# A two-block transformer on one core: tiles moved to multiples of 512 bytes in a partition

## The chip, the core and the metric

The kernel runs on one core of one Trainium2 chip. The metric is the device time of one execution in microseconds (us). The kernel before was timed three times: 1878.39 us median, 1877.34 to 1884.4 us.

Five engines are spoken of: PE (TensorE, matrix products), DVE (VectorE), ACT (ScalarE), POOL (GpSimd) and SP (SyncE, which here only issues loads). A tile in SBUF has 128 partitions; its address in this text is the byte at which it begins within a partition, and its *residue* is that address modulo 512.

## What is computed

256 tokens of 1024 channels pass through two blocks of two layers each, all in float32. Cut to what matters:

```
# first block: h = rms_norm(x) * (1 + scale(c)) + shift(c);  x = x + gate(c) * layer(h)
#   layer 0  retention:   q, k, v, g = split(h @ ret_w_in);  ... @ ret_w_out
#   layer 1  forgetting attention, 16 heads:  split(h @ fox_w_in);  ... @ fox_w_out
# second block: x = layer_norm(alpha * x + layer(x)) * g + b
#   conformer conv:  a, gate = split(x @ w_in);  u = a * sigmoid(gate)
#                    silu(layer_norm(depthwise_conv(u, 31 taps) + b)) @ w_out
#   dense ffn:       (silu(x @ w_gate) * (x @ w_up)) @ w_down               # 1024 -> 2816 -> 1024
#   short conv:      b, c, h = split(x @ w_in);  (b * depthwise_conv(c * h, 3 taps)) @ w_out
#   experts:         gates = softmax over the 2 chosen of 8 experts
#     for e in range(8):
#         h = silu(x @ w_gate[e]) * (x @ w_up[e])                           # 1024 -> 3584
#         out = out + gates[..., e:e+1] * (h @ w_down[e])                   # 3584 -> 1024
```

Of some 500 MB that are read, 352 MB are the weights of the eight experts (8 x 3 x 1024 x 3584 x 4 bytes).

## The kernel before

**Streamed weights.** The class `Stream` loads the weights in the order of their use, in units of 1 MB (a raw tile of 128 x 2048 float32), into rings of buffers. Each unit is split into two tiles of type fp32r, whose sum is the float32 value: ACT copies raw to `wH` with rounding (L122), DVE subtracts, `wL = raw - wH` (L123). There are three buffers of each. In the experts ten raw buffers run ahead: three in each of the pools "w", "w2" and "moe0" and one more.

**Three passes for a product.** `mm3` (L231 to L233) issues three matmuls for every product of 128 x 128 by 128 x N: high by high, low by high, high by low. A matmul has a *stationary* operand of 128 columns (512 bytes in each partition), which PE loads with LDWEIGHTS, and a *moving* operand of N columns that streams past it. In the profile's rows `mm<-wH,xg` the moving operand stands first, the stationary second. Each matmul of `mm3` loads its own stationary operand.

**Which operand is stationary** is decided by the stage. In `proj_wst` the weights are (`mm<-hH,wH`, N = 256). In the others the activations are, and the weights move with N = 512: `hH`, `hL` (first projections), `roH`, `foH` (outputs of the first block), `cR` (output of the conformer), `gH`, `gL` (dense down-projection), `soH`, `soL` (output of the short conv), and in the experts `xg`, `hT` or `hH` for gate and up, and `mhH`, `mhL` for down. The tokens of expert e lie in the tile `("xg", "hT", "hH")[e % 3]` (L1329): `xg` in the pool "moe" for experts 0, 3 and 6, the long-lived tiles `hT` and `hH` for the other five.

**One step of the experts** is 512 of the 3584 inner columns: 24 matmuls for the gate, 24 for up, 24 for down (of the columns before) and 4 transposes; there are 7 steps in each of 8 experts, and a step takes in six units. Between two experts `slots_back` carries rows back to their tokens. A second pass over the experts, under a condition, isn't run with these inputs.

**Where tiles lie.** Nothing in the kernel says an address. Pools lie behind each other in the order in which they are opened, and tiles within a pool in the order in which they are first asked for, each size rounded up to 32 bytes. So the sizes of the small tiles of the pool `cp` (`cv` L433, `cst` L436, `v` L475) set where every later pool begins, and small tiles at the start of "conf" (`cst`, L1099) and "moe0" (`rl`, `rmask`, `rpos` in `router_tiles`) set where the tiles behind them begin. Addresses of the built program, with the residue in brackets:

```
tile                                    address (residue)
cst (constants; identity at its start)  17824 (416)
x                                       23680 (128)
raw in "w", "w2", "tmp"                 40064 (128) and on, all 128
wH, wL                                  64640 (128) and on, all 128
hT, hH, hL, xn                          113792 (128) and on, all 128
roH, roL, foH, foL                      189056 (128), 167040 (128) and on, all 128
gH, gL                                  183424 (128) and on, all 128
cR (three buffers)                      183616 (320), 192832 (320), 202048 (320)
cW (three buffers)                      211264 (320), 215360 (320), 219456 (320)
oh, identR, raw in "moe0"               179552 (352), 181600 (352), 183136 (352) and on
soH, soL                                207712 (352), 215904 (352)
xg, ohT, mhH, mhL                       209760 (352), 217952 (352), 221024 (352), 225120 (352)
fxT, fv, fp, fpT (attention)            192, 64, 192 and 320 modulo 512
```

**What sets the order.** A scheduler orders the instructions of each engine by dependence and by the order of the code; loads keep the order of their units on SP's queue, and a load is issued once its raw buffer is free.

Of the kernel before, what the change touches and what calls it, by code (L numbers as in the profile page):

```python
# [6 lines left out]
F32 = mybir.dt.float32  # L7
# [7 lines left out]
P = 128  # L15
# [50 lines left out]
class Stream:  # L66
    """Weights in the order of their use: 1 MB loads run ahead as far as the rings of raw tiles
    allow, then each is split exactly into two parts that fp32r passes carry."""

    def __init__(self, K, split_bufs, pieces=2):  # L70
        self.K, self.SB, self.pieces = K, split_bufs, pieces
        self.units, self.raws, self.parts = [], {}, {}
        self.rings = []
        self.i = self.nl = self.ns = 0
        self.native = None
        self.side = {}
        self.after = 0      # units whose split stays behind what has been traced so far

    def beside(self, fn):
        """fn issues loads of its own in front of the next unit's."""  # L80
        self.side.setdefault(len(self.units), []).append(fn)

    def ring(self, pool, tag, bufs, upto=1 << 30):
        """Buffers for the raw units before unit upto."""
        self.rings.insert(0, [pool, tag, bufs, 0, upto])
# [50 lines left out]
    def ahead(self, n, behind=True):  # L136
        """Splits the next n units, behind what has been traced so far."""
        self.after = max(0, self.i + n - self.ns) if behind else 0
        self._split(self.i + n)

    def get(self, key, hold=0):
        """The next unit; hold: units got before that are still to be used."""
        k, _, split = self.units[self.i]
        assert k == key, (k, key)
        if self.native is not None:
            self.native[3] -= 1
            self.native = None
        self._split(self.i + 1)
        ahead = 0
        j = self.i + 1  # L150
        while j < len(self.units) and ahead < self.SB - 1 - hold:
            ahead += self.units[j][2]
            j += 1
        self._split(j)
        self._load()
        r = self.parts.pop(self.i)
        self.i += 1
        if not split:
            self.native = r[1]
            return r[0]  # L160
        return r
# [31 lines left out]
class Kern:  # L193
# [9 lines left out]
    def table(self, func, after):  # L203
        """Has ACT load func's table off the critical path, once `after` is there."""
        self.nc.scalar.activation(self.t(self.sp, [P, 1], "tab", bufs=2), after, func)

    def ld(self, dst, src):
        """A load that keeps its place among those of the weights."""
        self.tc.keep_in_program_order(self.nc.sync.dma_start(out=dst, in_=src))

    def soon(self, n=400):
        """What is traced inside goes ahead of work traced up to n instructions before."""
        return self.tc.high_priority(n)
# [21 lines left out]
    def behind(self, ins, prev):  # L235
        """ins goes after prev on their engine."""
        self.tc.add_manual_dep(ins.ins, prev.ins.name,
                               mybir.DependencyInfo(mybir.DependencyClass.NoSync, mybir.DependencyReason.DATA),
                               reason="order")

# [1 line left out]
    def proj_tok(self, key, after=None, begun=False):  # L242
        """[t, 512] per token tile, from two units of four k blocks; begun: by first_tok."""
# [11 lines left out]
    def first_tok(self, key):  # L255
        """The first token tile's part of the first unit of a phase."""
# [4 lines left out]
    def proj_wst(self, key, hH, hL):  # L261
        """[n, t] for two blocks of 128 n, from one unit of eight k blocks."""
# [9 lines left out]
    def first_half(self, key):  # L272
        """The first token tile's part of a phase's first product, which needs nothing of the second tile."""
        self.fps = self.mm()
        self.fw = self.st.get(key, 2)
        self.first_tile(0)
# [11 lines left out]
    def proj_two(self, key, key2, begun, between):  # L288
        """Two products as of proj_wst; between takes the first, returns the second. begun: by first_half."""
# [20 lines left out]
    def out_k2(self, key, acc, oH, oL, ks, first, last):  # L310
        """acc[tt][nh] += o[k block].T @ w rows, one unit of two k blocks; oH(k, tt) an AP."""
# [8 lines left out]
    def out_k4(self, key, acc, oH, oL, ks, nh, first, last):  # L320
        """The same for one half of n, one unit of four k blocks."""
# [7 lines left out]
    def out_last(self, key, acc, oH, oL, parts):  # L329
        """The last two units of a product, a token tile at a time; parts: (k blocks, nh, first, last) of each."""  # L330
# [32 lines left out]
    def rpow(self, src, n, eps, scale=1.0, tag="rstd"):  # L363
        """(src * scale + eps) ** -0.5 for a [128, n] AP."""
# [7 lines left out]
    def ln_stats(self, parts, eps):  # L372
        """mean and rstd ([128, 1] each) over the free axis of a list of [128, 512] APs."""
# [11 lines left out]
    def new_h(self, f=True, parts=True):  # L385
        """Channels by tokens, [128, 8, 256]: f32 and the two parts of it."""
# [4 lines left out]
    def turned(self, x, tt, nh):  # L391
        """x.T of one token tile and half of the channels: [128, 4, 128] in a bank."""
# [8 lines left out]
    def plain(self, x, tt):  # L401
        """Token tile tt of x into hT or hH and hL."""
# [9 lines left out]
    def affine(self, x, tt, A, B, f, H, L, func=AF.Identity):  # L412
        """func(A*x.T + B) of token tile tt, and its parts; A, B: [128, 8]."""
# [16 lines left out]
    def setup(self, tmp):  # L430
        nc, a = self.nc, self.a
        cp = self.cp
        cv = cp.tile([P, 8], F32, name="cv")  # L433
        nc.scalar.dma_start(out=cv, in_=a["c"].rearrange("o (p k) -> p (o k)", k=8))
        self.x = self.t(self.xp, [P, 2, DM], "x", bufs=2)
        self.c = c = cp.tile([P, C_MAIN], F32, name="cst")  # L436
# [33 lines left out]
    def vectors(self):  # L470
        """The vectors along partitions."""
# [3 lines left out]
        self.v = self.cp.tile([P, 2 * P], F32, name="v")  # L475
        self.nc.vector.tensor_copy(self.v, ps[:, 0:2 * P])
# [9 lines left out]
    def mod_start(self, parts):  # L486
        """Bias of four chunks of 512 columns, one per 32 partitions, and the sums' bank."""
# [20 lines left out]
    def shift_scale(self, m, i):  # L508
        """m: chunks shift lo, shift hi, scale lo, scale hi -> A = g*(1+scale), B = shift, [128, 8]."""
# [13 lines left out]
    def gate_row(self, m, i):  # L523
        """m: chunks gate0 lo, hi, gate1 lo, hi -> row i spread over the partitions, [128, 1024]."""
# [9 lines left out]
    def residual(self, acc, gate, tt):  # L534
        """x + gate * acc of token tile tt, and rsqrt of its mean square."""
# [216 lines left out]
    def fox(self):  # L752
# [3 lines left out]
        with self.tc.tile_pool(name="fox", bufs=1) as fp:  # L756
# [11 lines left out]
            def decay(ps):  # L768
                """log forget gates, [t, 16] per token tile."""
# [24 lines left out]
            def running(lf):  # L794
                """Their running sums."""
# [14 lines left out]
            def qk(key, g, is_q, begun=False):  # L810
                """Normed heads with the decay's columns: [t, head, 64 | 2] per token tile."""
# [30 lines left out]
            gq, gk = self.v[0:66, P + 24:P + 25], self.v[0:66, P + 25:P + 26]  # L842

            def stage_t(d):
                """Transposed q and k of one head, with the gains."""
# [35 lines left out]
            def stage_v(d0, d1):  # L881
                """o.T of two heads into oT[:, pair, :]."""
# [87 lines left out]
    def rows(self, g, b):  # L970
        """Vectors along the free axis, spread over the partitions."""
# [5 lines left out]
    def deepnorm(self, acc, gb, first, f=False, parts=True):  # L977
        """x = LN(alpha*x + acc)*g + b and its transposed parts; first() follows those of the first token tile."""
# [26 lines left out]
    def conv_rows(self):  # L1005
        """Tap rows by tap mod 4, the upper half of the channels 32 partitions further on, and the
        first 256 channels' as they are from partition 64 on."""
# [11 lines left out]
    def conv_weights(self):  # L1019
        """Taps as [tap mod 4 and channel, group of 32 channels, tap block], and by channel, [128, 2, 31]."""  # L1020
# [14 lines left out]
    def conformer(self):  # L1035
        nc = self.nc
        hH, hL = self.hH, self.hL
        with self.tc.tile_pool(name="conf", bufs=1) as cp:
# [60 lines left out]
            st = self.t(cp, [P, 2, 4, 6], "cst", bufs=1)  # L1099
# [10 lines left out]
            def taps_apart(k, js):  # L1110
                """A block of channels, tap by tap."""
# [76 lines left out]
    def short_conv(self):  # L1188
        nc = self.nc
        hH, hL = self.hH, self.hL  # L1190
        with self.tc.tile_pool(name="sc", bufs=1) as sp:
            oH = sp.tile([P, 8, T], F32R, name="soH")
            oL = sp.tile([P, 8, T], F32R, name="soL")
            wv = self.v[:, P:P + 24].rearrange("p (j k) -> p j k", j=3)
# [29 lines left out]
    def router_tiles(self, pool):  # L1224
        t = lambda n, *sh: pool.tile([P, *sh], F32, name=n)
        self.rl = t("rl", 2, 8)
        self.rt = t("rmask", 2, 8), t("rpos", 3, 8)
        self.oh = self.t(pool, [P, 2, 2, P], "oh", F32R, bufs=1)

    def route(self, tt):  # L1230
        """Router of one token tile: which two experts."""
# [27 lines left out]
    def slots(self, tt):  # L1259
        """The slots of one token tile in the first two experts."""  # L1260
# [15 lines left out]
    def counts(self):  # L1276
        """Tokens of each expert."""
# [15 lines left out]
    def route_weights(self, pool):  # L1293
        """Softmax over the two chosen logits, zero elsewhere; the largest count as an integer."""
# [23 lines left out]
    def gather_steps(self, es, base, oh=None, bank=None):  # L1318
        """Slots base..base+127 of the tokens of two experts: transposed parts per expert, and
        the one-hot rows that carry slots back to tokens; five steps, the last yields them."""  # L1320
# [34 lines left out]
    def experts(self, st, base):  # L1355
        """All experts over their slots base..base+127; adds their gated rows to self.o."""
# [46 lines left out]
        def down_last(e, HL):  # L1403
            """The last rows of the last expert, half of the columns at a time."""
# [25 lines left out]
        def slots_back(e, nh, yHL):  # L1430
            """The slots' rows at their tokens, of half of the columns."""
# [18 lines left out]
        def dense_gates():  # L1450
            """The first gates of the first expert, for all tokens: needs no routing."""
# [12 lines left out]
        def dense_gather(h, HLs):  # L1464
            """The rows of the first expert's slots."""
# [55 lines left out]
    def rest(self):  # L1521
        """Gates, alpha * x and the largest count."""
# [117 lines left out]
    def startup(self):  # L1640
        """The first block's input, half of the channels at a time, and with each half the products that it allows."""
# [143 lines left out]
```

## Time and profile before

| | |
|---|---|
| median of three runs | 1878.39 us (1877.34 to 1884.4) |
| the profiled execution, first to last instruction | 1873.6 us |
| PE busy | 1809.3 us (97%) |
| DVE busy | 1415.0 us (76%) |
| ACT busy | 1064.7 us (57%) |
| mean granted clock of TensorE | 0.986 |
| HBM read | 504.28 MB, 270 GB/s over the span |
| the experts, from their first product to the last | 824 to 1859 us |

The profiled execution is 4.8 us shorter than the median; what lies before the first and behind the last instruction is in the median and not in the span.

How to read it: busy time of PE is made of ends that are modelled, so a matmul's own duration tells little of how fast matmuls follow each other. That is read from their starts in the timeline: the start of the last of a run of matmuls, less the start of the first, by the number of gaps between them. In the timeline a column is the start, the next the modelled duration.

### The profile page before, as it was taken

Reading aid. Unit: us, or ns where it says so; the run is one execution under the profiler, and the core shown is the slowest. Engines: PE = TensorE matmul, PEld = TensorE weight load, DVE = VectorE, ACT = ScalarE, POOL = GpSimd, SP = SyncE. Lnnn points to the kernel's source line nnn. Section 1 sums busy time; section 2 is a strip of 40 time slices with the busy share of each in tenths; the row PEclk is TensorE's granted clock in tenths of the full one; section 3 lists DMA queues with packets and bytes.
Section 4 is the critical chain, followed back from the end, with each engine's and each line's share of the span. In section 5 each row is a group of like instructions: output and inputs, shape, how many; then the busy total and the mean of one; then the engine's idle time right before and its main releaser. Section 6 shows DMA issues by size and latency. Waiting matters only on the chain. (4 is left out here: it accounts for less than half of the span.)

```text
span 1873.6 us, 24361 instructions
## 1 busy us (share of the span) xinstructions
PE 1809.3 (97%) x9741; PEld 1486.5 (79%) x9741; DVE 1415.0 (76%) x1469; ACT 1064.7 (57%) x1036; POOL 65.7 (4%) x112
## 2 busy tenths in 40 slices
PE   6999999999999999999999999999999999999996
PEld 3867778789689998987878878878778788788785
DVE  3656666667775557679888888888888888888887
ACT  3333445654443433347767767767767677677673
POOL 1000003001100001000000000000000000000000
PEclk9999999999999999999999999999999999999998
DMA  9677646237356557548999989999999999999991
GB/s 356 233 274 243 224 141 202 77 113 252 114 180 190 188 184 243 195 147 316 346 359 340 362 297 363 369 340 337 349 319 365 360 342 355 316 349 366 332 365 68
DMA packets 252615, 509.34 MB, mean 272 GB/s; under 512 B 12347, under 2 KB 68782, under 8 KB 251470
## 3 DMA queue, kind: packets, MB, share of 16 engines
q1 hardware_dynamic: 249550, 500.64, 76.3%
q0 software_dynamic: 2592, 6.97, 1.2%
q8 instruction: 78, 1.28, 0.3%
q14 instruction: 43, 0.35, 0.1%
q10 hardware_dynamic: 352, 0.10, 0.0%
HBM read 504.28 MB, written 1.05 MB: 270 GB/s over the span
## 5 line engine op out<-in xcount | busy, mean ns | idle before, releaser
L123 DVE TENSOR_TENSOR wL<-raw,wH 128x2048 fp32r<-128x2048 f32 (+2 forms) x582 | 1033.9, 1801 | 258.7 <-ACT wH L122 257.6
L122 ACT CAST wH<-raw 128x2048 fp32r<-128x2048 f32 (+2 forms) x582 | 870.4, 1517 | 466.4 <-PE mm L233 144.3
L231 PE MATMUL mm<-hH,wH 128*128 128x256 f32 x816 | 232.2, 285 | 0.0
L232 PE MATMUL mm<-hL,wH 128*128 128x256 f32 x816 | 231.6, 284 | 0.0
L233 PE MATMUL mm<-hH,wL 128*128 128x256 f32 x816 | 231.2, 283 | 0.3 <-DVE wL L123 0.3
L231 PE MATMUL mm<-wH,hH 128*128 128x512 f32 (+1 forms) x512 | 200.4, 393 | 4.9 <-ACT wH L122 2.6
L232 PE MATMUL mm<-wL,hH 128*128 128x512 f32 (+1 forms) x512 | 199.4, 389 | 1.0 <-DVE wL L123 1.0
L232 PE MATMUL acc<-wL,mhH 128*128 128x512 f32 x448 | 178.5, 399 | 0.0
L233 PE MATMUL acc<-wH,mhL 128*128 128x512 f32 x448 | 176.6, 394 | 0.0
L231 PE MATMUL acc<-wH,mhH 128*128 128x512 f32 x448 | 166.8, 395 | 0.0
L231 PEld LDWEIGHTS mm<-hH,wH 128*128 128x128 f32 x816 | 156.5, 192 | 5.4 <-ACT wH L122 2.5
L233 PEld LDWEIGHTS mm<-hH,wL 128*128 128x128 f32 x816 | 156.5, 192 | 1.4 <-DVE wL L123 1.3
L232 PEld LDWEIGHTS mm<-hL,wH 128*128 128x128 f32 x816 | 156.6, 192 | 0.6 <-issue 0.2
L231 PE MATMUL mm<-wH,hT 128*128 128x512 f32 x336 | 133.1, 396 | 3.5 <-DVE x L1446 3.5
L231 PE MATMUL mm<-wH,xg 128*128 128x512 f32 x328 | 131.0, 399 | 3.5 <-DVE x L1446 3.5
L232 PE MATMUL mm<-wL,hT 128*128 128x512 f32 x336 | 132.7, 395 | 0.4 <-DVE wL L123 0.4
L233 PE MATMUL mm<-wH,hT 128*128 128x512 f32 x336 | 132.0, 393 | 0.0
L232 PE MATMUL mm<-wL,xg 128*128 128x512 f32 x328 | 130.8, 399 | 0.1
L233 PE MATMUL mm<-wH,xg 128*128 128x512 f32 x328 | 130.0, 396 | 0.0
L231 PEld LDWEIGHTS mm<-wH,hH 128*128 128x128 f32 x512 | 98.2, 192 | 30.9 <-ACT wH L122 3.6
L232 PEld LDWEIGHTS mm<-wL,hH 128*128 128x128 f32 x512 | 98.3, 192 | 21.7 <-DVE wL L123 3.5
L233 PE MATMUL mm<-wH,hL 128*128 128x512 f32 (+1 forms) x288 | 110.9, 385 | 0.7 <-DVE hL L361 0.7
(376 smaller groups left out, 2422.6 us busy)
## 6 DMA issues: line engine op xcount, KB each, us to landing
raw<-in_moe_w_gate_dram SPq DMA_DIRECT2D x112, 1024.0 KB
raw<-in_moe_w_up_dram SPq DMA_DIRECT2D x112, 1024.0 KB
raw<-in_moe_w_down_dram SPq DMA_DIRECT2D x111, 1024.0 KB
raw<-in_ret_w_in_dram SPq DMA_DIRECT2D x24, 1024.0 KB
raw<-in_mod_w_dram SPq DMA_DIRECT2D x32, 512.0 KB
raw<-in_fox_w_in_dram SPq DMA_DIRECT2D x16, 1024.0 KB
raw<-in_sc_w_in_dram SPq DMA_DIRECT2D x12, 1024.0 KB
raw<-in_ffn_w_gate_dram SPq DMA_DIRECT2D x11, 1024.0 KB
```

What stands on the lines that cost most here:

```text
L122: ops = (K.nc.scalar.copy(H[:, s], raw[:, s]), K.nc.vector.tensor_tensor(L[:, s], raw[:, s], H[:, s], op=ALU.subtract))
L123: K.nc.vector.tensor_tensor(L[:, s], raw[:, s], H[:, s], op=ALU.subtract))
L231: self.mm_first = mmul(ps, sH, mH, start=first, stop=False)
L232: mmul(ps, sH, mL, start=False, stop=False)
L233: self.mm_last = mmul(ps, sL, mH, start=False, stop=last)
```

## The change

The instructions and their order on every engine stay as they are, but for one: the copy of the transposed vectors out of PSUM writes 2 x 32 columns instead of 256. All else that changes is the size of four tiles, one tile that nothing uses (`rpad`), and with these the addresses. Comments and docstrings are taken out too, which moves line numbers by one to three; these and unchanged hunks are left out here.

```diff
     def setup(self, tmp):
...
-        cv = cp.tile([P, 8], F32, name="cv")
+        cv = cp.tile([P, 32], F32, name="cv")[:, 0:8]
...
-        self.c = c = cp.tile([P, C_MAIN], F32, name="cst")
+        self.c = c = cp.tile([P, 640], F32, name="cst")[:, 0:C_MAIN]
...
     def vectors(self):
...
-        self.v = self.cp.tile([P, 2 * P], F32, name="v")
-        self.nc.vector.tensor_copy(self.v, ps[:, 0:2 * P])
+        self.v = self.cp.tile([P, 2 * P // 4], F32, name="v")
+        self.nc.vector.tensor_copy(self.v.rearrange("p (i n) -> p i n", i=2),
+                                   ps[:, 0:2 * P].rearrange("p (i n) -> p i n", i=2)[:, :, 0:32])
...
-            gq, gk = self.v[0:66, P + 24:P + 25], self.v[0:66, P + 25:P + 26]
+            gq, gk = self.v[0:66, 56:57], self.v[0:66, 57:58]
...
-            st = self.t(cp, [P, 2, 4, 6], "cst", bufs=1)
+            st = self.t(cp, [P, 128], "cst", bufs=1)[:, 0:48].rearrange("p (a b c) -> p a b c", a=2, b=4)
...
-            wv = self.v[:, P:P + 24].rearrange("p (j k) -> p j k", j=3)
+            wv = self.v[:, 32:56].rearrange("p (j k) -> p j k", j=3)
...
     def router_tiles(self, pool):
         t = lambda n, *sh: pool.tile([P, *sh], F32, name=n)
         self.rl = t("rl", 2, 8)
+        t("rpad", 72)
         self.rt = t("rmask", 2, 8), t("rpos", 3, 8)
```

In the built program all tiles of the table above then have the residue 0 (x at 23040, wH at 64000, cR at 183296, xg at 209408, mhH at 220672), but for the attention's fxT, fv, fp and fpT, which go to 64, 448, 64 and 192.

## Rows read from the trace of the kernel before

**Rows 1.** The page: the span, busy time by engine, and DMA in 40 slices

```profile
span 1873.6 us, 24361 instructions
PE 1809.3 (97%) x9741; PEld 1486.5 (79%) x9741; DVE 1415.0 (76%) x1469; ACT 1064.7 (57%) x1036; POOL 65.7 (4%) x112
DMA  9677646237356557548999989999999999999991
```

**Rows 2.** Busy time by stretch: length, engines' busy time (count), PE clock, DMA share, GB/s

```profile
1200.00:1400.00 200.00, 194.38 (x865) 156.05 (x864) 169.21 (x110) 138.32 (x100) 0.00 (x0) 0.99 0.96 340
1400.00:1600.00 200.00, 197.40 (x903) 161.72 (x902) 172.91 (x105) 143.36 (x103) 0.00 (x0) 1.00 0.99 354
1171.00:1218.00 47.00, 47.00 (x213) 38.51 (x212) 41.24 (x23) 34.12 (x23) 0.00 (x0) 1.00 1.02 370
```

**Rows 3.** Who waited for whom, 1000 to 1600 us: us in total, times, longest

```profile
PE mm L231 <- DVE x L1446: 5.3, 3, 1.8
PE mm L1437 <- ACT hL L358: 3.4, 4, 0.9
PE mm L1437 <- DVE mhL L361: 1.5, 1, 1.5
PE mm L232 <- DVE wL L123: 0.4, 1, 0.4
...
SPq L209 <- DVE wL L123: 467.0, 187, 6.5
```

**Rows 4.** Timeline of PE, first and last of unbroken runs: start, modelled us, instruction

```profile
1163.25 0.39 PE L231 MATMUL mm<-wH,hH 128*128 128x512 f32 x1
...
1173.90 0.40 PE L233 MATMUL mm<-wH,hH 128*128 128x512 f32 x1
...
625.22 0.40 PE L231 MATMUL acc<-wH,gH 128*128 128x512 f32 x1
...
635.90 0.39 PE L233 MATMUL acc<-wH,gL 128*128 128x512 f32 x1
...
1271.66 0.40 PE L231 MATMUL mm<-wH,xg 128*128 128x512 f32 x1
...
1282.63 0.39 PE L233 MATMUL mm<-wH,xg 128*128 128x512 f32 x1
...
868.58 0.39 PE L231 MATMUL acc<-wH,mhH 128*128 128x512 f32 x1
...
873.95 0.39 PE L233 MATMUL acc<-wH,mhL 128*128 128x512 f32 x1
...
514.17 0.40 PE L231 MATMUL acc<-wH,cR 128*128 128x512 f32 x1
...
533.53 0.40 PE L233 MATMUL acc<-wH,cR 128*128 128x512 f32 x1
...
568.25 0.28 PE L231 MATMUL mm<-hH,wH 128*128 128x256 f32 x1
...
591.16 0.28 PE L233 MATMUL mm<-hH,wL 128*128 128x256 f32 x1
```

**Rows 5.** Groups of PE by line and form, with their count

```profile
L231 PE MATMUL mm<-hH,wH 128*128 128x256 f32 x816 | 232.2, 285 | 0.0
...
L232 PE MATMUL acc<-wL,mhH 128*128 128x512 f32 x448 | 178.5, 399 | 0.0
...
L231 PE MATMUL mm<-wH,xg 128*128 128x512 f32 x328 | 131.0, 399 | 3.5 <-DVE x L1446 3.5
...
L1090 PE MATMUL mm<-cR,cW 128*32 128x256 f32 x384 | 21.7, 380 | 0.0
...
L231 PE MATMUL acc<-wH,cR 128*128 128x512 f32 x32 | 13.4, 419 | 0.0
...
L231 PE MATMUL acc<-wH,soH 128*128 128x512 f32 x32 | 12.7, 398 | 0.0
```

**Rows 6.** The splits of raw tiles, 1000 to 1600 us: duration ns min/median/max

```profile
L122 ACT CAST wH<-raw x199: 1896/1913/1933, 998.4 to 1598.9; 128x2048 fp32r<-128x2048 f32 x199
L123 DVE TENSOR_TENSOR wL<-raw,wH x198: 2279/2291/2296, 1000.3 to 1596.5; 128x2048 fp32r<-128x2048 f32 x198
```

**Rows 7.** The copy of the transposed vectors: duration ns, start

```profile
L476 DVE COPY v<-acc x1: 417/417/417, 49.2 to 49.2; 128x256 f32<-128x256 f32 x1
```

## The prediction, made before the changed kernel was run

> **What bounds the kernel now.** The page comes first: PE is busy for 97% of the span [rows 1]. A busy PE need not be the bound, since the ends of its matmuls are modelled, so the waits are next: in 600 us of the experts PE waits 10.6 us in all, at the borders between experts, and only 0.4 us for a split of weights [rows 3]. Nor do loads hold anything up there: SP waits 467 of the 600 us for a split to free a raw buffer [rows 3], so the loads stand ready before their buffers do. DMA is near its end all the same: a share of 0.96 to 0.99 at 340 to 354 GB/s over 200 us [rows 2]. So PE is the bound, DMA stands close behind it, and what one matmul takes from start to start is what the kernel takes, some 8,000 times over.
>
> That number is not read from the durations but from starts in the timeline [rows 4]. Each pair there is the first and the last matmul of a run without a break:
> - `hH` stationary (residue 128): 48 matmuls, 1163.25 to 1173.90, 47 gaps in 10.65 us: 226.6 ns.
> - `gH`, `gL` (128): 48 matmuls, 10.68 us: 227.2 ns.
> - `xg` (352): 48 matmuls, 10.97 us: 233.4 ns.
> - `mhH`, `mhL` (352): 24 matmuls, 23 gaps in 5.37 us: 233.5 ns.
> - `cR` (320): 84 matmuls, 83 gaps in 19.36 us: 233.3 ns.
> - `wH`, `wL` stationary (128), N = 256: 192 matmuls, 191 gaps in 22.91 us: 119.9 ns.
>
> The moving weights of the N = 512 runs lie at 128 in all of them, so the two classes differ in the stationary operand. It isn't the region of SBUF: `gH` (from 183424) and `cR` (from 183616) overlap. It isn't the engine that wrote the tile or the stage: `xg` and `hH` are filled by the same lines and multiplied by the same lines. What is left is the residue: 320 and 352 are not multiples of 128 bytes, 128 is. The 6.5 ns (233.4 less the mean of 226.6 and 227.2) are a cost per stationary load.
>
> **The change part by part.** *Stationary tiles at 320 or 352 go to 0.* The matmuls of `mm3` with such a tile, by the counts of the groups [rows 5]: `xg` 3 x 328 = 984, `mhH` and `mhL` 3 x 448 = 1344, `cR` 3 x 32 = 96, `soH` and `soL` 3 x 32 = 96 (each row shown is one of three of its kind), 2,520 in all. No row shows a stationary fp32r tile at 0; the nearest are those at 128, since 0 too is a multiple of 128 bytes, and I take their price: 2,520 x 6.5 ns = 16.4 us. PE has no other work to hide the loss and none to absorb the gain, for it does not wait inside these runs [rows 3], so all of it is on the path.
>
> *Tiles at 128 go to 0.* That is all other stationary operands of `mm3`: 3 x 816 with N = 256 [rows 5], and with N = 512 some 3,000 (`hH`, `hT`, `hL`, `gH`, `roH`, `foH` and their partners, counted in the same view), with the short runs some 5,500 in all. What could they gain? 256 more columns cost 226.6 - 119.9 = 106.7 ns, which is 2.4 columns a ns, the upper of the clock's two levels. So streaming costs 106.7 ns of the 119.9, and 13.2 ns are fixed, with N = 512 as with N = 256. The bounds are a gain of all 13.2 ns (73 us) and a loss of 6.5 ns (36 us, as at 352). I take nothing: 13.2 ns are 32 columns' time, the same at both N, which looks like a fixed change of weights and not like a read that misses its line; at 320 and 352 it is half as much again.
>
> *Raw, wH, wL and the other operands of ACT and DVE.* Of the raw tiles split between 1000 and 1600 us a third lie at 352 and the rest at 128, and yet the copies take 1896 to 1933 ns and the subtractions 2279 to 2296 [rows 6]: no second group, so the residue costs these engines nothing. I take 0; were the spread of 17 ns in the subtraction all residue, it would be hidden behind PE, which does not wait for splits.
>
> *Loads* write to other addresses. Between the residues 128 and 352 the trace shows no load that PE waits for [rows 3], so a cheaper one gives nothing at once. It is the cover that matters, below.
>
> *Smaller things.* `cW` goes from 320 to 0: 384 matmuls with 32 stationary columns [rows 5], at 6.5 ns each at most 2.5 us, but four run beside each other; I take 0. `ohT` and the transposes of `mh`: 64 and 224 matmuls, at most 1.9 us, part of it inside the stalls between experts; 0. Identity to 0 and the attention's tiles to 64, 192 or 448: these are float32 matmuls in stages with stalls; 0. The copy of `v` takes 417 ns [rows 7] and writes a quarter: less than 0.4 us, at 49 us, where PE has not settled; 0.
>
> *What is late next.* Each step of the experts becomes 24 x 6.5 = 0.16 us shorter with `hT` or `hH` and 0.47 us with `xg`. Over the experts that is 15 of some 1,035 us, so the feed must rise by 1.5%, from about 345 to about 350 GB/s. 200 us at 354 and 47 us at 370 GB/s [rows 2] say that it can.
>
> **Sum.** The profiled execution has a span of 1873.6 us [rows 1], 4.8 us less than the median of 1878.4. Taken from the median: 1878.4 - 16.4 = 1862.0 us, 0.87% less.
>
> The Trainium skill speaks against any gain: in "SBUF — State Buffer", section Specifications (TRN2), it gives cachelines of 16 bytes and a penalty for each access that crosses to a new line. All of 0, 128, 320 and 352 are multiples of 16, so by this page the residues are alike and the time stays at 1878. The rows differ by 6.5 ns, so here the measurement decides against the page as the whole story.
>
> **The rivals.** *A: the residue of 128 costs too.* If the fixed 13.2 ns are partly a stationary load that begins off a multiple of 256 or 512, tiles at 0 lose half of it (6.6 ns, one more such step): 2,520 + 5,500 matmuls by 6.6 ns are 53 us on top, 1809 us. For it: the cost falls from 320 to 128, so why stop. Against: 320 and 352 cost the same, so it does not grow with the distance, and 13.2 ns appear as a round 32 columns. "TensorE: Matmul & The Clock Gate" of the Trainium skill, section Back-to-back issue gap, is on this rival's side: N / 2.4 + 2.5 ns, 215.8 ns for N = 512, where no run of the trace goes below 226.6.
>
> *B: the feed takes the gain.* PE gets faster, DMA doesn't, and PE begins to wait for splits: the time stays at 1878, or falls by a few us in the conformer and short conv alone (192 matmuls, 1.2 us). For it: DMA's share is 0.96 to 0.99 in the experts [rows 2]. Against: 370 GB/s in the stretch with the fastest steps, and loads that wait for buffers. That the 6.5 ns belong to something other than the residue, so that the change does nothing, gives the same time and its chance is counted with this rival; the page's rule above would be such a case.
>
> *C: slower.* If 0 is the bad place, for example since the stationary load, the moving weights and DVE's and ACT's tiles then all begin at the same residue of 512, every stationary operand at 128 pays what 352 pays now: 5,500 x 6.5 = 36 us, and the 2,520 gain nothing: 1914 us. It decides from the point where a matmul at 0 takes over 229.6 ns (16.4 us by 5,500 is 3 ns more than 226.6). Against: today hH, wH and wL all lie at 128, and this is the faster class.
>
> **How the numbers follow.** The forecast 0.65; A 0.12; B 0.16; C 0.07. The predicted time is the forecast's, 1862. Its own range is 1856 to 1870 (5 to 8 ns by 2,520 to 2,600, and the clock: the profiled execution has a mean granted clock of 0.986, so some us are spent at the lower level and can come or go). For 8 in 10 it takes in B, and a small part of A: 1848 to 1883; A's full size and C stay out. A measurement of this kernel can tell about 0.5%, 9.4 us, from no change: faster by more than that is nearly all of the forecast and A, 0.73; within it B and the poor end of the forecast, 0.20; slower is C, 0.07.
>
> **What would show it.** In the timeline of the changed kernel: gaps of 226.6 to 227.2 ns with `xg`, `mhH`, `cR` and `soH` stationary (233 means that the residue was not the cause); gaps of 120 ns in `proj_wst` unchanged (lower is A, higher C); the busy time by stretch at about 350 GB/s in the experts; among the waits still no PE wait for `wH` or `wL` (many would be B); the split's durations unchanged. The forecast is wrong if the gaps fall as said and the span doesn't: then the waits name what took it.

## The result, and the profile after

The changed kernel takes 1857.86 us (median of four runs, 1856.31 to 1860.5), the kernel before 1878.29 in the same comparison: a ratio of 0.9885, 95% interval 0.9865 to 0.9905. Two later comparisons gave 0.9916 (0.9898 to 0.9934) and 0.9908 (0.9888 to 0.9929). The prediction of 1862.0 us holds in sign and size. The reason that it gave for the 6.5 ns does not, as the experiments show.

The page of the changed kernel, the lines that answer to [rows 1]:

```profile
span 1857.2 us, 24361 instructions
PE 1792.8 (97%) x9741; PEld 1484.4 (80%) x9741; DVE 1413.6 (76%) x1469; ACT 1065.0 (57%) x1036; POOL 65.7 (4%) x112
...
DMA  9677645327455556647999989999999999899992
```

The span fell by 16.4 us and PE's busy time by 16.5, DVE's and ACT's stayed. That this is just the forecast sum is in part luck: the two profiled executions have mean granted clocks of 0.986 and 0.990, which by the slope given below is worth some 5 us. The timeline of PE, first and last matmul of unbroken runs (start, modelled us, instruction), as in [rows 4]; line numbers below 470 are those of before:

```profile
1155.84 0.39 PE L231 MATMUL mm<-wH,hH 128*128 128x512 f32 x1
...
1166.49 0.39 PE L233 MATMUL mm<-wH,hH 128*128 128x512 f32 x1
...
1206.24 0.39 PE L231 MATMUL mm<-wH,xg 128*128 128x512 f32 x1
...
1216.89 0.39 PE L233 MATMUL mm<-wH,xg 128*128 128x512 f32 x1
...
866.41 0.39 PE L231 MATMUL acc<-wH,mhH 128*128 128x512 f32 x1
...
871.63 0.39 PE L233 MATMUL acc<-wH,mhL 128*128 128x512 f32 x1
...
512.48 0.39 PE L232 MATMUL acc<-wL,cR 128*128 128x512 f32 x1
...
531.77 0.39 PE L233 MATMUL acc<-wH,cR 128*128 128x512 f32 x1
...
566.61 0.28 PE L231 MATMUL mm<-hH,wH 128*128 128x256 f32 x1
...
589.53 0.28 PE L233 MATMUL mm<-hH,wL 128*128 128x256 f32 x1
```

`hH`: 47 gaps in 10.65 us, 226.6 ns, as before. `xg`: 47 gaps in 10.65 us, 226.6, was 233.4. `mhH`, `mhL`: 23 gaps in 5.22 us, 227.0, was 233.5. `cR`: 85 gaps in 19.29 us, 226.9, was 233.3. `proj_wst`: 191 gaps in 22.92 us, 120.0, unchanged. Tiles that went from 128 to 0 gained nothing; tiles that went from 320 or 352 to 0 gained all that they had lost.

The waits of PE from 1000 to 1600 us (in total, times, longest), and busy time by stretch (length, engines, clock, DMA share, GB/s), as in [rows 2, 3]:

```profile
PE mm L231 <- DVE x L1448: 5.3, 3, 1.8
PE mm L1439 <- ACT hL L358: 3.4, 4, 0.9
PE mm L1439 <- DVE mhL L361: 1.5, 1, 1.5
PE mm L232 <- DVE wL L123: 0.4, 1, 0.4
```

```profile
1200.00:1400.00 200.00, 194.34 (x882) 158.89 (x881) 172.01 (x112) 140.34 (x102) 0.00 (x0) 0.99 0.96 345
1400.00:1600.00 200.00, 197.40 (x909) 162.94 (x908) 173.61 (x106) 144.20 (x102) 0.00 (x0) 1.00 0.99 358
```

PE waits for the same things as long as before. In the same 400 us it starts 882 and 909 matmuls where it started 865 and 903, and the loads follow: 345 and 358 GB/s, were 340 and 354. No split became late.

### The profile page after: what moved, and what is told of

Read it like the earlier page. It is cut to its first block, busy times and chain, and to the rows that moved or that the text cites. A ratio compares the mean times of both kernels' runs of the same rounds, so it can differ in the third digit from the quotient of the medians.

```text
span 1857.2 us, 24361 instructions
## 1 busy us (share of the span) xinstructions
PE 1792.8 (97%) x9741; PEld 1484.4 (80%) x9741; DVE 1413.6 (76%) x1469; ACT 1065.0 (57%) x1036; POOL 65.7 (4%) x112
```

## The experiments

Two theories explain the first result alike. **Line:** a stationary operand costs 6.5 ns if its address is no multiple of 128 bytes (the prediction). **Pair:** what counts is how the addresses of stationary and moving operand lie to each other; in the kernel before, the fast class had both at 128 and the slow class had 320 or 352 against 128. In the changed kernel every pair lies at 0 and 0. The theory of the pair was formed only after the first four kernels below, so their expectations speak of the first alone.

A table at the end of this section has all times side by side. The runs of one kernel in one comparison scatter by up to 13 us (before: 1873.4 to 1886.3), and much of that follows the mean granted clock that the row of the core names. The 48 runs of the kernel before give 1.2 us for each 0.001 of that clock (seven runs at 0.990 have a mean of 1873.4 us, nine at 0.984 one of 1879.6). The last column of that table brings the mean of each kernel to 0.987 by this slope, and "at the same clock" below means that column. Brought to 0.987 in this way, single runs of before still lie some 2 us to either side, and the means of before in the four comparisons run from 1875.1 to 1877.3: differences of 1 to 2 us in that column are noise.

### Only the two small paddings

```diff
--- before
-            st = self.t(cp, [P, 2, 4, 6], "cst", bufs=1)
+            st = self.t(cp, [P, 64], "cst", bufs=1)[:, 0:48].rearrange("p (a b c) -> p a b c", a=2, b=4)
...
         self.rl = t("rl", 2, 8)
+        t("rpad", 8)
```

> The kernel before with 24 floats of padding in two places: 16 behind the small tile of conf and 8 in moe0 (rpad of 8, not 72). The tiles of conf and moe0 and all behind them go from 320 and 352 to 384; everything else stays at 128, and the copy of v stays as it was. Theory (only a stationary address that is no multiple of 128 bytes costs; 128 and 0 are alike): 2,520 matmuls lose 6 to 6.5 ns, 15 to 16.4 us less than before, 1862 us by the median, and the profiled span equals that of the changed kernel (1857) within 2 us; gaps with xg, mhH, cR 227 ns. Rival 1 (multiples of 512 matter too, and gave the 4 us by which the median fell more than the gaps explain): 4 us above the changed kernel. Rival 2 (part of the gain came from elsewhere in the change: DMA writes, identity, v): 1865 to 1878.

Measured: 1864.45 us, ratio 0.9936 (0.9917 to 0.9955); the profiled span is 1856.3 us, and the gaps with `xg` are 227 ns:

```profile
1205.10 0.39 PE L231 MATMUL mm<-wH,xg 128*128 128x512 f32 x1
...
1215.76 0.39 PE L233 MATMUL mm<-wH,xg 128*128 128x512 f32 x1
```

24 floats of padding give the whole gain: at the same clock 1861.7 us, against 1861.1 for the changed kernel. Multiples of 512 are not needed, and neither the copy of `v` nor the places of raw and identity have a part in it. Both theories allow this: 384 is a multiple of 128, and 384 and 128 are alike modulo 256.

### The changed kernel again

> The changed kernel once more, in more rounds and beside the others on the same chip. Theory: 16.4 us below before (the sum of the gaps, and the difference of the two profiled spans); the 20.4 us between the two medians of the first comparison is scatter. Rival: 20 us again, which means that some 4 us come from something that the gaps do not show.

Measured: 1862.07 us, 0.9916 (0.9898 to 0.9934), 15.0 us below before by the medians, and 15.0 at the same clock, over all three comparisons. So the 20.4 us of the first comparison most likely had some 5 us of clock in them: its four runs had 0.987 to 0.990, the profiled run of before 0.986 (the clock of its other runs is not on record). Two profiled runs of this same kernel, with the same mean gap of 227.3 ns, differ by 6 us:

```profile
core 0: 1857.2 us, clock 0.990
```

```profile
core 0: 1863.3 us, clock 0.986
```

### Every large tile at 64

```diff
--- changed kernel
-        cv = cp.tile([P, 32], F32, name="cv")[:, 0:8]
+        cv = cp.tile([P, 48], F32, name="cv")[:, 0:8]
```

> The changed kernel with 16 more floats behind cv, so that all large tiles lie at 64 modulo 512 and not at 0. Theory (every stationary load at no multiple of 128 bytes costs 6 to 6.5 ns): some 8,000 matmuls of mm3 pay, of these some 5,500 with N = 512 and 2,450 with N = 256: 48 to 52 us more than the changed kernel, 1906 to 1910 us; gaps 233 ns at N = 512 and 126 at N = 256. Rival 1 (only N = 512 pays, N = 256 has the load hidden): 33 to 36 us more, 1891 to 1894. Rival 2 (the moving operand, raw or the operands of DVE and ACT pay as well): over 1915, with splits longer than 1916 and 2291 ns. Rival 3 (64 is as good as 0; the bad places are those above 256): 1858.

Measured: 1859.17 us, 0.9901 (0.9879 to 0.9924). `xg` at 64, weights at 64:

```profile
1208.34 0.39 PE L231 MATMUL mm<-wH,xg 128*128 128x512 f32 x1
...
1219.00 0.39 PE L233 MATMUL mm<-wH,xg 128*128 128x512 f32 x1
```

47 gaps in 10.66 us, 226.8 ns. The theory of the line forecast 233 and a loss of some 50 us, and got neither: it falls here. 64 is no multiple of 128, and it costs nothing when the moving operand lies at 64 too. By itself this run fits the third rival too, that the bad places are those above 256; the sweep below has slow places from 32 on, and `mh` at 64 was slow as well.

### A sweep of places, by itself

```python
def run(st, mv, n=48):
    for j in range(n):
        nc.tensor.matmul(ps[0:st.shape[-1], 0:w], st, mv, start=j == 0, stop=j == n - 1)
for i in range(16):
    run(s[i][:, 0:128], m[:, 0:512])              # stationary at 32*i
...
for i in range(16):
    run(s[0][:, 0:128], m[:, 8 * i:8 * i + 512])  # moving at 32*i
```

> A kernel of its own, which computes nothing of the reference: runs of 48 fp32r matmuls with one stationary tile of 128 columns, which is loaded anew each time, at residues 0, 32, 64, ... 480 (tiles sa to sp), with N = 512, 256 and 128; then the moving operand moved in steps of 32 bytes with the stationary at 0; then a stationary of 64 columns. Theory: start to start 227 ns (N = 512) and 120 ns (N = 256) at 0, 128, 256 and 384, and 6 to 6.5 ns more at all other residues; no difference between moving residues. With N = 128 the same steps, unless the load itself is then the bound. Rival 1 (a step at every 64 bytes or a cost that grows with the distance from the line): several levels. Rival 2 (the moving operand pays too): a step in the sweep of the moving operand. Rival 3 (512 matters in a kernel without other traffic): 0 alone is fastest.

Measured, start to start with N = 512: 226.7 ns with the stationary at 0 and at 256, and at no other of the 16 places; 229.0 at 192 and 448, 232.5 to 234.2 at the rest, 128 and 384 among them (232.5). The first and last matmul of the runs at 128 (`se`) and 256 (`si`), 47 gaps each:

```profile
73.32 0.39 PE L38 MATMUL acc<-m,se 128*128 128x512 f32 x1
...
84.25 0.39 PE L38 MATMUL acc<-m,se 128*128 128x512 f32 x1
...
117.87 0.39 PE L38 MATMUL acc<-m,si 128*128 128x512 f32 x1
...
128.53 0.40 PE L38 MATMUL acc<-m,si 128*128 128x512 f32 x1
```

With the moving operand moved instead, again 0 and 256 alone have 226.7 to 226.9, and 64 and 320 have 228.9, the mirror of 192. So no operand is at fault by itself: it is how the two lie to each other, with a period of 256 bytes. At N = 128 all places lie between 110.5 and 111.7 ns.

The last sweep, with a stationary operand of 64 columns, sets a limit to this. There equal places are not the best: 230 ns at 0 and 256, and 226.7 at 96 and 352 alone (N = 512; 228.3 to 232.7 at the rest). The runs at 0 (`sa`) and 96 (`sd`):

```profile
584.26 0.39 PE L38 MATMUL acc<-m,sa 128*64 128x512 f32 x1
...
595.08 0.40 PE L38 MATMUL acc<-m,sa 128*64 128x512 f32 x1
...
617.60 0.39 PE L38 MATMUL acc<-m,sd 128*64 128x512 f32 x1
...
628.25 0.39 PE L38 MATMUL acc<-m,sd 128*64 128x512 f32 x1
```

So what counts is the difference of the two places, and which difference is the best depends on the matmul's form too. Why, no run here shows.

### The weights against the rest

```diff
--- changed kernel
+                if not self.ns:
+                    K.wpool.tile([P, 16], F32, name="wpad0")
                 H = K.wpool.tile([P, 2048], F32R, tag="wH", name=f"wH{self.ns}", bufs=self.SB)
                 L = K.wpool.tile([P, 2048], F32R, tag="wL", name=f"wL{self.ns}", bufs=self.SB)
+                if not self.ns:
+                    K.wpool.tile([P, 16], F32, name="wpad1")
```

> The changed kernel with 16 floats ahead of the first wH and 16 behind the first wL: wH and wL lie at 64 modulo 512, all that comes behind them (hT, hH, hL and on) at 128, the identity and x at 0. New theory (a matmul is fast if the stationary operand that is loaded beside it and the moving operand have the same address modulo 256; the address alone doesn't matter): all some 5,450 matmuls of mm3 with N = 512 (moving 64, stationary 128, difference +64) pay 6 to 6.6 ns, 33 to 36 us; those with N = 256 (stationary 64, moving 128, difference -64, as 192) get faster, 120.0 to 117.8 ns, 2,448 of them, 5 us: in sum 28 to 31 us more than the changed kernel, 1887 to 1892 us. Old theory (a stationary operand at no multiple of 128 costs): only the 2,448 with wH and wL stationary pay, 126 ns, 15 to 16 us: 1874 to 1878. Rival (64 is as good as 0 for every tile, whatever the other lies at): 1860.

The built program is not what this text says: both paddings came to lie behind `wL`, so `wH` and `wL` stayed at 0 and all that lies behind them went to 128. This tells the theories apart still better. All places are multiples of 128, so by the line nothing costs anything and the time is 1858 to 1862. By the pair the difference is 128, and the sweep gave 232.5 for that. These two numbers were not on record before the run.

Measured: 1889.72 us, slower than before, 1.0072 (1.0048 to 1.0096). `xg` at 128 with weights at 0; then `wH` at 0 stationary, `hH` at 128 moving (lines are four further down):

```profile
1223.20 0.39 PE L235 MATMUL mm<-wH,xg 128*128 128x512 f32 x1
...
1234.13 0.39 PE L237 MATMUL mm<-wH,xg 128*128 128x512 f32 x1
...
571.10 0.28 PE L235 MATMUL mm<-hH,wH 128*128 128x256 f32 x1
...
594.01 0.29 PE L237 MATMUL mm<-hH,wL 128*128 128x256 f32 x1
```

47 gaps in 10.93 us, 232.6 ns, in the very tiles that the theory of the line holds to be in good places. The run with N = 256 has 191 gaps in 22.91 us, 119.9 ns; those in the conformer took 118.7. Over all matmuls the mean is 232.5 (N = 512) and 119.1 (N = 256), against 227.3 and 119.9 in the changed kernel: some 5,470 by 5.2 ns less some 2,500 by 0.8 are 26.4 us; at the same clock the kernel is 24.9 us slower than the changed one.

### The change without its two paddings

```diff
--- changed kernel
-            st = self.t(cp, [P, 128], "cst", bufs=1)[:, 0:48].rearrange("p (a b c) -> p a b c", a=2, b=4)
+            st = self.t(cp, [P, 48], "cst", bufs=1)[:, 0:48].rearrange("p (a b c) -> p a b c", a=2, b=4)
...
-        t("rpad", 72)
```

> The changed kernel without the two paddings of conf and moe0: raw, wH, wL, hT, hH, gH and all up to there at 0, as in the changed kernel; cR at 192 and xg, mhH, mhL, soH at 224. New theory: the differences of stationary and moving operand modulo 256 are those of the kernel before (0, and 192 and 224), so no gain at all: 1874 to 1878 us, gaps of 233 ns with xg, mhH and cR. Old theory: the same time. Rival (part of the gain is from 512-byte places of raw, wH, wL and the copy of v): 3 us or more below before.

Measured: 1877.3 us, 1.0002 (0.9987 to 1.0018): no gain, though raw (but for that of moe0), `wH`, `wL`, `hH`, `gH` lie at multiples of 512. With the first experiment this divides the change: the paddings in front of conf and moe0 are all of it. One group went another way: `cR`, with the same difference of 192 as in the kernel before, took 233.3 ns there [rows 4] and here 86 gaps in 19.69 us, 229.0:

```profile
514.01 0.39 PE L231 MATMUL acc<-wH,cR 128*128 128x512 f32 x1
...
533.70 0.40 PE L233 MATMUL acc<-wH,cR 128*128 128x512 f32 x1
```

### Every pair of places

Two kernels of their own, in the order of `mm3`: the first with `hH` and `wH` moved alone and together, and bf16; the second with all pairs.

```python
for d in range(8):
    for o in range(8):
        tok(8 * o, 8 * d)    # stationary at 32*o, moving at 32*d bytes; N = 512
for d in range(8):
    for o in range(8):
        wst(8 * o, 8 * d)    # the same with N = 256
```

> A kernel of its own, which computes nothing of the reference: 48 matmuls for each setting in the order of mm3 (high by high, high by low, low by high), four tiles at multiples of 512 bytes. First mm<-wH,hH as in proj_tok, N = 512, with the stationary operand begun 0, 32, ... 224 bytes into its tile; then acc<-wH,hH as in proj_wst, N = 256, with the moving operand begun 0, 32, ... 224 bytes in; then N = 512 with the stationary 4, 8, ... 28 bytes in, and with both operands 4, 8, ... 28 bytes in; last bf16 with N = 512 and the stationary 0, 32, ... 224 bytes in. New theory: N = 512: 227 ns at difference 0 and 231 to 234 at all others, 233 at 192 and 224 as in the kernel before; at 4 to 28 bytes slow too; with both operands moved alike 227. N = 256: 120.0 at 0 and 117 to 120 elsewhere, least for a moving operand at 160 (stationary less moving 96). Rival (only multiples of 32 bytes are seen, so 4 to 28 are fast): 227 there. bf16: the weight load is half as many bytes; no forecast.

> A kernel of its own, which computes nothing of the reference: runs of 48 matmuls in the order of mm3 with every pair of places: stationary at 0, 32, ... 224 by moving at 0, 32, ... 224 (modulo 256; the moving place changes slowest), first all 64 pairs with N = 512 as in proj_tok, then all 64 with N = 256 as in proj_wst. Theory D (only the difference of the two places counts): the same time along each diagonal, 226.7 ns on the diagonal of equal places and 229 to 234 off it; with N = 256 120.0 on the diagonal and 117.5 to 119.7 off it. Rival P (the places count by themselves too): with stationary 64 and moving 128 the kernel before took 233.1 ns, with 192 and 0 the run without the paddings of conf and moe0 took 229.2, the same difference; P expects these two numbers again, D expects one number in both.

Two of the 64 pairs with N = 512 in the timeline of the second kernel, stationary 64 with moving 0, and both at 128:

```profile
49.28 0.40 PE L34 MATMUL mm<-wH,hH 128*128 128x512 f32 x1
...
54.65 0.39 PE L36 MATMUL mm<-wH,hL 128*128 128x512 f32 x1
...
427.90 0.39 PE L34 MATMUL mm<-wH,hH 128*128 128x512 f32 x1
...
433.11 0.40 PE L36 MATMUL mm<-wH,hL 128*128 128x512 f32 x1
```

23 gaps each: 5.37 us, 233.5 ns, and 5.21 us, 226.5 ns. The 64 pairs by their difference, stationary less moving modulo 256; each number is the mean of eight pairs, from the starts:

```
difference      0     32     64     96    128    160    192    224
N = 512     226.8  233.2  233.4  234.2  232.6  233.4  229.0  233.4
N = 256     119.8  118.3  116.8  118.0  118.6  119.8  117.8  117.6
```

With N = 512 the eight pairs of a difference agree within 0.8 ns (D): stationary 64 with moving 128 takes 228.8 here, not the 233.1 of the kernel before (P). With N = 256 equal places are the slowest, together with a difference of 160, and a few pairs leave their diagonal: stationary 160 with moving 96 takes 113.8, most others with the difference 64 take 117.8. In the first kernel, both operands moved alike by 4 bytes take 237.7 ns, by 8 bytes 232.0, by 28 bytes 229.2, where 227 had been expected: equal places help only at multiples of 32 bytes, of which the grid has all. The stationary alone moved by 4 to 28 bytes takes 229.9 to 235.0, slow as expected. With N = 256 and the stationary at 0, a moving operand at 160 was expected to be the fastest: the first kernel gave 118.7 there and 117.8 to 117.9 at 32, 64 and 192, the second 117.3 at 160. And bf16 takes 215.8 at each of eight places of the stationary operand.

### One term alone

```diff
--- changed kernel
             HLs = []
+            self.t(mp, [P, 16], "mpad", bufs=1)
```

> The changed kernel with a tile of 16 floats that nothing uses ahead of mhH in the pool moe: mhH and mhL lie at 64 modulo 512, all else as in the changed kernel (the moving weights at 0). In the run with all tiles at 64 these same two lay at the same 64, with the weights at 64 too, and their matmuls took 227 ns. Theory D: 1,344 matmuls at 233.3 ns and not 227.3, 8.1 us more than the changed kernel (1866 to 1870 us), xg, hT, hH as before at 227. Rival (64 is a good place for a stationary tile, wherever the moving one lies): no change, 1858 to 1862, and gaps of 227.

Measured: 1869.89 us, 0.9945 (0.9925 to 0.9965); at the same clock 8.2 us above the changed kernel, where 1,344 matmuls by 5.8 ns are 7.8. `mhH` at 64, then `xg` at 0, weights at 0:

```profile
869.96 0.40 PE L231 MATMUL acc<-wH,mhH 128*128 128x512 f32 x1
...
875.33 0.40 PE L233 MATMUL acc<-wH,mhL 128*128 128x512 f32 x1
...
1212.96 0.39 PE L231 MATMUL mm<-wH,xg 128*128 128x512 f32 x1
...
1223.62 0.39 PE L233 MATMUL mm<-wH,xg 128*128 128x512 f32 x1
```

23 gaps in 5.37 us, 233.5 ns, and 47 in 10.66, 226.8. The same tile at the same 64 took 227 ns where the weights lay at 64 too. Nothing but the place of these tiles against the weights differs between the two.

### Unequal places where N is 256

```diff
--- changed kernel
-        self.hH = self.t(self.hp, [P, 8, T], "hH", F32R, bufs=1) if parts else None
-        self.hL = self.t(self.hp, [P, 8, T], "hL", F32R, bufs=1) if parts else None
+        o = (0, 24) if f else (40, 0)
+        self.hH, self.hL = [self.t(self.hp, [P, 8 * T + w], n, F32R, bufs=1)[:, i:i + 8 * T].rearrange("p (k t) -> p k t", k=8)
+                            if parts else None for n, w, i in (("hH", 40, o[0]), ("hL", 24, o[1]))]
```

> The changed kernel, and in the conformer, the dense ffn and the short conv the tiles hH and hL, which there only move, begin at 160 modulo 256 (40 floats into the tile), with the stationary wH and wL at 0: stationary less moving is 96. Wherever hH and hL are stationary they stay at 0. The built program has 1,872 matmuls with N = 256 at this pair of places. By the grid of the kernel bench3 they take 117.4 ns and not 119.9: 4.7 us less than the changed kernel, 1853 to 1857 us where that takes 1858 to 1862; N = 512 unchanged at 227. Rival (beside ACT, DVE and loads the mode of the bench is not kept): gaps of 118.3 to 120, 0 to 3 us.

The second version has `(0, 16) if f else (48, 0)`, paddings of 48 and 16, and `cv` with 72 columns.

> The same with other places: 40 more floats behind cv bring all large tiles to 160 modulo 256, and in the conformer, the dense ffn and the short conv hH and hL begin at 96: stationary less moving is 64. In the grid the pair of stationary 160 and moving 96 settled into 113.3 ns after four matmuls, other pairs with the difference 64 at 117.8. So 1,872 matmuls by 2.1 to 6.5 ns: 4 to 12 us less than the changed kernel. Rival (the mode at 113.3 is lost at every change of the weight tile): 117.8, 4 us.

> The changed kernel beside the two on the same chip, to compare them with; 15 to 20 us below before, as twice already.

Measured in one comparison: 1860.72 us (0.991, 0.9887 to 0.9932) with the difference 96, 1857.19 us (0.9893, 0.9873 to 0.9914) with 64, 1859.44 us (0.9908, 0.9888 to 0.9929) for the changed kernel. The intervals overlap; at the same clock the first is 2.1 us and the second 6.4 us below the changed kernel, the first of which is hardly more than the noise. The gaps say more: with 96 they are 118.6 ns over 1,858 gaps. The 117.4 ns and the time of 1853 to 1857 us that were expected did not come; 118.6 is within the rival's 118.3 to 120, and it is what the first of the two kernels above gave for this very pair (118.7). With 64 they are 115.7, in two kinds, within the 113.4 to 117.8 that were expected; 1,872 matmuls by 1.3 and by 4.2 ns are 2.4 and 7.9 us. A run in the dense ffn with the difference 96, 191 gaps in 22.67 us:

```profile
568.98 0.28 PE L231 MATMUL mm<-hH,wH 128*128 128x256 f32 x1
...
591.65 0.28 PE L233 MATMUL mm<-hH,wL 128*128 128x256 f32 x1
```

The timeline of the second, a run in the dense ffn and one in the conformer, at the same places:

```profile
568.28 0.28 PE L231 MATMUL mm<-hH,wH 128*128 128x256 f32 x1
...
590.78 0.28 PE L233 MATMUL mm<-hH,wL 128*128 128x256 f32 x1
...
447.95 0.28 PE L232 MATMUL mm<-hL,wH 128*128 128x256 f32 x1
...
480.38 0.28 PE L233 MATMUL mm<-hH,wL 128*128 128x256 f32 x1
```

191 gaps in 22.50 us are 117.8 ns, 286 gaps in 32.43 us are 113.4. One pair of places has two speeds, and a long run keeps the one that it falls into. In this execution all five runs of the dense ffn took 117.8 and the long ones of the conformer and the short conv 113.4; with the weights at 0 and the rest at 128, one run of the dense ffn took 118.6 and the other four 120.0. That `cR` took 233.3 once and 229.0 the other time may be the same; no run here shows what decides it.

### All of them

| kernel | stationary, moving mod 256 (N = 512) | mean gap N = 512, 256 (ns) | median us | mean us at clock 0.987 |
|---|---|---|---|---|
| before | 128, 128; 96 or 64, 128 | 227.3; 233.2, 119.9 | 1875.7 to 1881.6 | 1876.1 |
| changed | 0, 0 | 227.3, 119.9 | 1857.9, 1862.1, 1859.4 | 1861.1 |
| only the paddings | 128, 128 | 227.3, 119.9 | 1864.4 | 1861.7 |
| all at 64 | 64, 64 | 227.3, 119.9 | 1859.2 | 1862.8 |
| weights 0, rest 128 | 128, 0 | 232.5, 119.1 | 1889.7 | 1886.0 |
| without the paddings | 0, 0; 224 or 192, 0 | 227.4; 233.2 (`cR` 229.2), 119.9 | 1877.3 | 1876.2 |
| `mh` at 64 | 0, 0; 64, 0 | 227.4; 233.1, 119.9 | 1869.9 | 1869.3 |
| N = 256 at 96 | 0, 0 | 227.3, 118.6 (moved tiles) | 1860.7 | 1859.0 |
| N = 256 at 64 | 160, 160 | 227.3, 115.7 (moved tiles) | 1857.2 | 1854.7 |

## Why the prediction was right, and where it was not

**What bounds the kernel:** right. What the gaps lost or gained showed in the time, within 1.5 us, in five kernels and in both directions: the changed one (14.9 by the gaps, 15.0 at the same clock), weights against the rest (26.4 and 24.9), `mh` (7.8 and 8.2), and the two with N = 256 (2.4 and 2.1, 7.9 and 6.4). One reading beside it needs a correction: the 4.8 us between the median before and the profiled span are not all outside the instructions. In every run with both numbers on record the time exceeds the span by 1.7 to 1.9 us (1858.98 and 1857.2); the other 3 us are scatter between executions. The sum takes its gain from the median, so it does not change.

**The term of 16.4 us:** right in size, a little too large. The means of all gaps are 233.2 and 227.3, which is 5.9 ns and not the 6.5 of the cleanest runs: 2,520 by 5.9 are 14.9 us. That the first comparison came out at 20.4, still within the range, is most likely scatter of the clock.

**The cause:** wrong. The step that failed is "What is left is the residue: 320 and 352 are not multiples of 128 bytes, 128 is". The sentence ahead of it, that the moving weights lie at 128 in all runs, was taken as a reason to leave them out. It should have been read the other way: where one operand never moves, its place can't be told from a fixed line, and the slow class was the one whose place differed from the weights'. The number came out by luck: the change moves both operands to 0, so that line and pair give the same sum. With only one of the two moved (weights at 0, rest at 128) the step would have forecast 1862 where 1890 was measured.

**Tiles from 128 to 0 gain nothing:** right (226.6 and 120.0 again), so rival A fell. But the reading of the 13.2 ns as a "fixed change of weights" fell for N = 256, which came down to 113.4 by the places alone. With N = 512 no fp32r run was below 226.5, not with 64 stationary columns either, and what these 13 ns are stays open.

**Rival B:** the loads rose from 354 to 358 GB/s and PE waited no longer for them. In "SBUF — State Buffer" of the Trainium skill, section Specifications (TRN2), cachelines of 16 bytes would make all of these places alike; the grid has 226.8 to 234.2 ns among multiples of 32, and the measurement decides. **Rival C** took the equal places of all operands for a danger; with N = 512 and 128 stationary columns they are the very condition of the fast class.

**The rest:** raw tiles and splits at nothing is right; from 1000 to 1600 us the changed kernel has

```profile
L122 ACT CAST wH<-raw x201: 1899/1916/1935, 1000.0 to 1596.7; 128x2048 fp32r<-128x2048 f32 x101
...
L123 DVE TENSOR_TENSOR wL<-raw,wH x202: 2279/2291/2296, 998.8 to 1599.5; 128x2048 fp32r<-128x2048 f32 x101
```

as in [rows 6] (the count at the end of a line is of a sample). The clock, for which the range left "some us", goes with 1.2 us for each 0.001 of its mean.

## What to carry to other kernels

Where fp32r matmuls with 128 stationary columns and N = 512 follow each other back to back, let the stationary and the moving operand begin at the same address modulo 256 bytes, and at a multiple of 32: 6 to 7 ns of 233 each, for a few floats of padding. Where N is 256 or the stationary operand has 64 columns, equal places cost more than the best pair, and the best pair has to be tried. And when a property separates fast from slow in a trace, ask which other operand had the same value in all rows: a single sweep of both, in a kernel of a millisecond, tells what no trace of the one kernel can.

## What the runs showed of the hardware that was not expected

- The difference of the two addresses modulo 256 sets the gap of fp32r matmuls with 128 stationary columns (N = 512: 226.7 at equal places, 229.0 at 192, 232.5 to 234.2 at the others), whatever the places themselves are at multiples of 32 bytes. One exception is open: `cR` in the kernel before, with a difference of 192, took 233.3.
- With 64 stationary columns the best difference is 96 (226.7 ns), and equal places take 230.
- One pair of places can have two speeds (113.4 and 117.8 ns, N = 256), and one of them lasts through a long run.
- bf16 at N = 512 has 215.8 ns at all eight places of the stationary operand, which are 384 matmuls in this group of the timeline (376 in the records; eight gaps are twice as long). Less the modelled 0.39 of the last one, 383 gaps take 82.66 us:

```profile
312.02 83.05 PE L66 MATMUL mm<-bw,bh 128*128 128x512 bf16 x376
```

  "TensorE: Matmul & The Clock Gate" of the Trainium skill, section Back-to-back issue gap, gives N / 2.4 + 2.5 ns, 215.8, as the isolated gap of a matmul, and for a stream with stationary loads some 131 ns at N = 512. The bf16 runs here, a stream with a stationary load each time, agree with the first figure and not with the second; fp32r, with its own stationary load each time, never came below 226.5 in an unbroken run.
